# One group of 32 small grams in place of two groups of 16

## The chip, the cores and the metric

The kernel runs on one core of a Trainium2 chip. Such a core has a matrix engine (TensorE, PE in the profile, PEld for its weight loads), a vector engine (VectorE, DVE), a scalar engine (ScalarE, ACT), GpSimd (POOL) and SyncE (SP), each with its own queue of instructions, and 16 DMA engines. The engines wait for each other by semaphores. TensorE writes into PSUM, eight banks of 128 x 512 numbers, from which VectorE and ScalarE read. The metric is the device time of one execution in microseconds.

## The reference

One block of a streaming encoder on 512 tokens of width 1024, in float32: half a SwiGLU network, then two token mixers side by side (RWKV-7 and an attention with forget gates) that are gated and added, then another half SwiGLU and a last norm. The change lies in the RWKV-7 mixer, whose state follows this rule, per head of 64 channels, 8 heads:

```python
def step(state, inp):
    r_t, w_t, k_t, v_t, a_t, b_t = inp
    sa = jnp.einsum('bhvk,bhk->bhv', state, a_t)
    state = (state * w_t[:, :, None, :]
             + sa[..., :, None] * b_t[:, :, None, :]
             + v_t[..., :, None] * k_t[:, :, None, :])
    y_t = jnp.einsum('bhvk,bhk->bhv', state, r_t)
    return state, y_t
```

with a = -kk and b = kk * a, and w a decay below one.

## The kernel before, in words

The step over tokens is computed in chunks of 32. Within a chunk, the products of every token's a and r with every earlier token's b and k are needed: a small matrix of 64 x 64 per chunk and head, here called a gram. The 8 heads are held as 4 pairs, p = 0 to 3, a pair being 128 partitions, head q of it 64. There are 16 chunks, so a pair has 32 grams. `BK` holds b and k of a pair, both divided by the running decay; `G[p][q]` holds a and r times the running decay in head q's own 64 partitions. A gram takes BK's and G's 64 partitions of head q and writes 64 partitions of a PSUM bank, those of the *other* head. Two banks `gps` (named gp in the profile) hold the 32 grams, bank g the chunks 8g to 8g + 7. A masking on VectorE then multiplies 8 grams by a triangular mask and puts the result into G, into the 64 partitions that head q does not use. So a pair has four maskings. Each gram is two passes on TensorE, and the grams of the two heads run side by side in it.

Around the grams, `step(p)` computes what they need: columns of the input projection (`column`, `plain_gate`), each 24 full-size passes of 128 x 512 (lines 143 to 145: the weights' high part by the input's high part, then by its low part, then the low part of the weights by the high part of the input). A column's weights are loaded by SP into one of three buffers (raw), ScalarE rounds them (whi, line 135), VectorE takes the rest (wlo, line 136); whi and wlo have two buffers each. A column's bank (pk, pgt, two of them in turn) is emptied by VectorE: u (line 1205) or, for a gate, gs (line 1235), which POOL then stores. k is shaped on VectorE from kt of ScalarE (line 1266). The norm of kk is a sum by TensorE (khi, klo into pn, lines 1281 and 1282) and three steps on ScalarE (krn). `rk` goes another such way: rhi and rlo into pn (lines 1334 and 1335), times v as bon (line 1337), a bias on ScalarE, a store by SP to bsave.

After its maskings, POOL copies a pair's strictly lower part to Ld in memory (line 1324) and clears it in G. When all four pairs are there, Ld is read back as Ls (line 1348), and VectorE inverts 128 triangular matrices of 32 x 32 at once by 31 steps of a product (prod, line 1358) and a sum (TT, line 1360). Meanwhile TensorE computes the columns of the attention: v (pv), two gates, q and k (pq). Then qk is scaled, squared (qsq), rounded (h), and the rest (l) goes with it into the next sum, again on TensorE.

The order of the work: up to the end of the inverse, the framework's scheduler sets each engine's order, from its own estimates of when each instruction can run; `tc.issue_after(x)` forbids an instruction to stand before x, and the text's order decides what depends on what. From there on (`written(True)`, line 1460) VectorE, ScalarE and TensorE follow the order in which the code is written.

Of the kernel before, what the change touches and what calls it, by code (L numbers as in the profile page):

```python
# [50 lines left out]
def kernel(  # L51
# [39 lines left out]
    def bank(name, pool_=None):  # L91
        pool_ = pool_ or pm
        return pool_.tile([P, T], F32, tag="b", name=name)
# [70 lines left out]
    def split(dst_hi, dst_lo, src, hi_eng="act"):  # L164
        cast = act.copy(dst_hi, src) if hi_eng == "act" else dve.tensor_copy(dst_hi, src)
        return cast, dve.tensor_tensor(dst_lo, src, dst_hi.bitcast(F32), op=ALU.subtract)
# [127 lines left out]
    def pc(i):  # L294
        return par[:, i:i + 1]
# [345 lines left out]
    class Wide:  # L641
# [240 lines left out]
        def column(s, ps):  # L882
            s.rc = s.small[4]
            for i in range(2):
                pe.transpose(ps[:, i * P:(i + 1) * P], s.nrm.rstd[:, i * P:(i + 1) * P], ident[:])
            for i in range(2):
                dve.tensor_copy(s.rc[:, i:i + 1], ps[:, i * P:i * P + 1])
# [183 lines left out]
    with ExitStack() as mx:  # L1071
# [119 lines left out]
        def prep(name, p, n=T):  # L1191
            if p % 2 == 0:
                return alt[name]
            t = t2.tile([P, n], F32, name=name, tag=name)
            return t[:]

        def work(name, dt=F32):
            late = name in ("kka", "rk", "bon")
            return t2.tile([P, T], dt, name=name, tag="sb" if late else "sa", bufs=3 if late else 5)
# [40 lines left out]
        def plain_gate(m):  # L1240
            gate = Gate(m)
            gate.go()
            gate.out()
            return gate.mms
# [3 lines left out]
        def step(p):  # L1248
            if p % 3 == 0:
                k, r = spare[2], spare[3]  # L1250
            else:
                k, r = [t2.tile([P, T], F32, name=f"{n}{p}")[:] for n in "kr"]
            v = vs[p]
            cz, a = za[p]
            BK = BKs[p]
            if p:
                column(DA, p, k, 4)
            kk = prep("kk", p)
            act.activation(kk[:], k[:], AF.Copy, scale=pc(PAR_KK + p))
            sq = work("ksq")  # L1260
            act.activation(sq[:], kk[:], AF.Square)
            hi, lo = work("khi", F32R), work("klo", F32R)
            split(hi[:], lo[:], sq[:])
            t = work("kt")
            act.activation(t[:], a[:], AF.Identity, bias=nka[:, p:p + 1], scale=pc(PAR_KA + p))
            dve.scalar_tensor_tensor(k[:], t[:], 1.0, k[:], op0=ALU.add, op1=ALU.mult)
            with tc.issue_after(after[-1].ins) if after else ExitStack():
                dve.tensor_tensor_scan(cz[:], cmask[:], cz[:], initial=0.0, op0=ALU.mult, op1=ALU.add)
            Pp = prep("Pp", p, NC * (C + 1)).rearrange("p (c t) -> p c t", t=C + 1)
            pool.memset(Pp[:, :, 0:1], 1.0)  # L1270
            Pi = prep("Pi", p)
            with tc.issue_after(logs.ins):
                act.activation(Pi[:], cz[:], AF.Exp, scale=DEC)
                act.activation(Pp[:, :, 1:C + 1], ch(cz), AF.Exp, scale=-DEC)
            pool.tensor_copy(PC[:, p, :], Pp[:, :, C])
            after.append(dve.tensor_tensor(BK[:, :, 1, :], ch(k), ch(Pi), op=ALU.mult))

            mms = column(0, p, r, 0) if p else spread
            ps = bank("pn", pf)
            with tc.issue_after(mms[2].ins):  # L1280
                pe.matmul(ps[:], bonesr[:], hi[:], start=True, stop=False)
                pe.matmul(ps[:], bonesr[:], lo[:], start=False, stop=True)
            rn = work("krn")
            act.activation(rn[:], ps[:], AF.Relu, bias=tiny[:, 1:2])
            with tc.issue_after(logs.ins):
                act.activation(rn[:], rn[:], AF.Ln, bias=tiny[:, 0:1])
            act.activation(rn[:], rn[:], AF.Exp, scale=-0.5)
            dve.tensor_tensor(kk[:], kk[:], rn[:], op=ALU.mult)
            ka = work("kka")
            dve.tensor_tensor(ka[:], kk[:], a[:], op=ALU.mult)  # L1290
            dve.tensor_tensor(BK[:, :, 0, :], ch(ka), ch(Pi), op=ALU.mult)
            for q in range(2):
                s = slice(q * 64, (q + 1) * 64)
                dve.scalar_tensor_tensor(G[p][q][s, :, 0, :], ch(kk)[s], -1.0, Pp[s, :, 0:C],
                                         op0=ALU.mult, op1=ALU.mult)
            for q in range(2):
                s = slice(q * 64, (q + 1) * 64)
                dve.tensor_tensor(G[p][q][s, :, 1, :], ch(r)[s], Pp[s, :, 1:C + 1], op=ALU.mult)
            column(2 * DA, p, v, 8)
            mms = plain_gate(p)  # L1300


            gps = [pr.tile([P, 8, 2, C], F32, tag="b", name="gp") for _ in range(2)]
            for a_ in range(2):
                with tc.issue_after(mms[5].ins):
                    for c in range(8):
                        for q in range(2):
                            g = (a_ + q) % 2
                            s = slice(q * 64, (q + 1) * 64)
                            o = slice((1 - q) * 64, (2 - q) * 64)  # L1310
                            cc = g * 8 + c
                            gm = pe.matmul(gps[g][o, c], BK[s, cc], G[p][q][s, cc], start=True, stop=True)
                for q in range(2):
                    g = (a_ + q) % 2
                    o = slice((1 - q) * 64, (2 - q) * 64)
                    dve.tensor_tensor(
                        G[p][q][o, g * 8:(g + 1) * 8].rearrange("p c a t -> p c (a t)"),
                        gps[g][o].rearrange("p c a t -> p c (a t)"),
                        gmask[o].rearrange("p a t -> p (a t)").unsqueeze(1).broadcast_to([64, 8, 2 * C]),
                        op=ALU.mult)  # L1320
            for q in range(2):
                r0 = (1 - q) * 64
                un = (q * NP + p) * NC
                nc.gpsimd.dma_start(Ld[un:un + NC].rearrange("c s t -> s c t"), G[p][q][r0:r0 + C, :, 0, :])
                pool.memset(G[p][q][r0:r0 + C, :, 0, :], 0.0)


            rk = work("rk")
            dve.scalar_tensor_tensor(rk[:], r[:], pc(PAR_RK + p), k[:], op0=ALU.mult, op1=ALU.mult)
            ps = bank("pn", pr)  # L1330
            hi, lo = work("rhi", F32R), work("rlo", F32R)
            split(hi[:], lo[:], rk[:])
            with tc.issue_after(gm.ins):
                pe.matmul(ps[:], bonesr[:], hi[:], start=True, stop=False)
                pe.matmul(ps[:], bonesr[:], lo[:], start=False, stop=True)
            bon = work("bon")
            dve.tensor_tensor(bon[:], ps[:], v[:], op=ALU.mult)
            act.activation(bon[:], bon[:], AF.Identity, bias=pc(PAR_LB + p))
            nc.sync.dma_start(bsave[p], bon[:])

        for p in range(NP):
            step(p)
# [797 lines left out]
```

## Time and profile before

| | us |
|---|---|
| median of 3 runs | 1101.12 (1100.97 to 1101.41) |
| the profiled execution | 1101.58 |
| its span, first to last instruction | 1099.8 |
| TensorE busy in the span | 1090.9 |
| VectorE, ScalarE, POOL busy | 839.4, 669.3, 212.0 |
| one masking (16 of them) | 0.69 |
| first and last gram start at | 398.7 and 461.9 |

Times within the execution are counted from the start of the span. In rows of single instructions stand the start, the length, the engine and line, the operation, what is written from what is read, the shape, and in brackets how long the engine sat idle before and what ended it. Matmuls are pipelined, so their lengths overlap: what a pass takes is the distance to the next start.

### The profile page before, as it was taken

To read this page: it belongs to the slowest core of one execution; us is meant where nothing else is said; L and a number is where in the kernel's file an instruction comes from. 1 tells how busy PE (TensorE), PEld (TensorE's weight loads), DVE (VectorE), ACT (ScalarE), POOL (GpSimd) and SP (SyncE) were. 2 spreads that over 40 slices of the span, in tenths; PEclk is the share of its full clock that TensorE was granted. 3 is DMA by queue.
4 is the path that set the end of the run, shared out by engine and by line. 5 is a ranking of instruction groups with operands and counts; after the bars stand their busy time and mean duration, and the time that the engine had idled before them with its cause. 6 is when DMAs were issued, how large, how long until landed. Compare 5 with 4: busy or idle time off the path is not lost.

```text
span 1099.8 us, 16207 instructions
## 1 busy us (share of the span) xinstructions
PE 1090.9 (99%) x6050; PEld 889.6 (81%) x6050; DVE 839.4 (76%) x1162; ACT 669.3 (61%) x1046; POOL 212.0 (19%) x255
## 2 busy tenths in 40 slices
PE   9999999999999999999999999999999999999997
PEld 7888888888887888888777777888888888888886
DVE  7997676789756699779877666877697766789874
ACT  6765556575555765346887766533586555576554
POOL 1211221134204112311000121112311202114210
PEclk9999999999999999999999999999999999999999
DMA  7979887879926334445212244544968888859982
GB/s 221 252 166 240 199 179 200 191 146 189 236 91 186 110 101 121 115 134 125 58 34 72 77 139 147 175 132 155 284 151 190 188 218 170 184 158 204 235 189 77
DMA packets 139724, 177.09 MB, mean 161 GB/s; under 512 B 9726, under 2 KB 75838, under 8 KB 139646
## 3 DMA queue, kind: packets, MB, share of 16 engines
q0 software_dynamic: 33328, 70.40, 33.6%
q1 hardware_dynamic: 105582, 104.21, 31.0%
q10 hardware_dynamic: 736, 1.45, 0.3%
q8 instruction: 48, 0.79, 0.3%
q14 instruction: 30, 0.25, 0.1%
HBM read 163.51 MB, written 12.52 MB: 160 GB/s over the span
## 4 chain that ended last, share of the span: by engine, by line
PE 97%; ACT 1%; DVE 1%; DMA 0%; issue 0%; DVEq 0%; ACTq 0%
PE P L71 39%; PE P L144 5%; PE P L145 5%; PE P L143 5%; PE pgt L71 5%; PE lp L71 3%; PE pq L71 2%; PE pk L145 2%; PE ppj L71 2%; PE pk L143 2%; PE pk L144 2%; PE pb L71 2%; PE pa L71 1%; PE pw L144 1%; PE pw L145 1%; PE pw L143 1%
## 5 line engine op out<-in xcount | busy, mean ns | idle before, releaser
L71 PE MATMUL P<-sraw,q 128*128 128x512 f32 x344 | 91.3, 389 | 0.0
L135 ACT CAST whi<-raw 128x1024 fp32r<-128x1024 f32 (+3 forms) x43 | 41.1, 956 | 65.4 <-issue 19.3
L71 PEld LDWEIGHTS P<-sraw,q 128*128 128x128 f32 x344 | 64.6, 188 | 13.4
L71 PE MATMUL P<-swhi,q 128*128 128x512 f32 x224 | 71.5, 390 | 0.0
L71 PE MATMUL P<-sraw,wxh 128*128 128x512 f32 x200 | 68.4, 394 | 0.0
L136 DVE TENSOR_TENSOR wlo<-raw,whi 128x1024 fp32r<-128x1024 f32 (+3 forms) x44 | 49.6, 1127 | 17.8 <-ACT whi L135 16.6
L71 PE MATMUL P<-swhi,wxh 128*128 128x512 f32 x144 | 56.9, 395 | 0.0
L71 PE MATMUL P<-swhi,wxl 128*128 128x512 f32 x144 | 56.1, 390 | 0.0
L71 PE MATMUL P<-swlo,wxh 128*128 128x512 f32 x144 | 56.1, 389 | 0.0
L684 POOL DMA_DIRECT2D cb<-in_ffn_w_dram x20 | 24.1, 1204 | 151.3 <-DVE cd L71 85.6
L71 PE MATMUL P<-sraw,wxl 128*128 128x512 f32 x136 | 53.0, 390 | 0.0
L71 PEld LDWEIGHTS P<-swhi,q 128*128 128x128 f32 x224 | 42.0, 188 | 9.1 <-DVE q L71 0.5
L684 POOL DMA_DIRECT2D cd<-in_ffn_w_dram x24 | 29.5, 1229 | 102.6 <-DVE swlo L71 38.1
L71 PE MATMUL P<-swlo,q 128*128 128x512 f32 x112 | 43.6, 389 | 0.0
L71 PEld LDWEIGHTS P<-sraw,wxh 128*128 128x128 f32 x200 | 37.2, 188 | 7.3
L71 ACT CAST sraw<-cd 128x1024 fp32r<-128x1024 f32 x30 | 31.5, 1050 | 15.1 <-PE P L71 11.5
L71 DVE TENSOR_TENSOR swlo<-ca,swhi 128x1024 fp32r<-128x1024 f32 x24 | 29.2, 1222 | 13.9 <-ACT swhi L71 13.9
L71 DVE TENSOR_TENSOR u<-P,u 128x512 f32<-128x512 f32 x52 | 34.1, 685 | 5.8 <-ACT u L71 5.7
L71 DVE TENSOR_TENSOR swlo<-cc,swhi 128x1024 fp32r<-128x1024 f32 x20 | 24.5, 1224 | 18.1 <-ACT swhi L71 17.8
L543 POOL DMA_DIRECT2D ca<-in_ffn_w_dram x16 | 19.3, 1205 | 96.4 <-DVE swlo L71 66.4
L143 PE MATMUL pk<-xh,whi 128*128 128x512 f32 x96 | 37.8, 394 | 0.0
L145 PE MATMUL pk<-xh,wlo 128*128 128x512 f32 x96 | 37.5, 391 | 0.0
(613 smaller groups left out, 3451.6 us busy)
## 6 DMA issues: line engine op xcount, KB each, us to landing
raw<-in_w_in_dram SPq DMA_DIRECT2D x40, 512.0 KB
cc<-in_ffn_w_dram SPq DMA_DIRECT2D x36, 512.0 KB
cb<-in_ffn_w_dram POOLq DMA_DIRECT2D x36, 512.0 KB, 6.0
cb<-in_ffn_w_dram SPq DMA_DIRECT2D x32, 512.0 KB
cd<-in_ffn_w_dram POOLq DMA_DIRECT2D x32, 512.0 KB, 7.6
ca<-in_ffn_w_dram POOLq DMA_DIRECT2D x32, 512.0 KB, 7.1
ca<-in_ffn_w_dram SPq DMA_DIRECT2D x20, 512.0 KB
cd<-in_ffn_w_dram SPq DMA_DIRECT2D x18, 512.0 KB
```

The source lines that it names most:

```text
L71: q.last = do(*a, **kw)
L135: (hi_eng or act).copy(hi[:], raw[:])
L136: (eng or dve).tensor_tensor(lo[:], raw[:], hi[:].bitcast(F32), op=ALU.subtract)
L143: pe.matmul(ps, whi, xhi, start=first, stop=False, skip_group_check=onto)
L144: pe.matmul(ps, whi, xlo, start=False, stop=False, skip_group_check=onto)
L145: return pe.matmul(ps, wlo, xhi, start=False, stop=last, skip_group_check=onto)
L543: nc.gpsimd.dma_start(s.sum[g], src, accum_op=ALU.add)
L684: nc.gpsimd.dma_start(to, s.block(b, n, h), accum_op=ALU.add)
```

## The change

In `step`, the loop over the two groups (a_ = 0 and 1) held 16 grams and the two maskings of these 16. It is cut in two: a first loop issues all 32 grams, a second all four maskings.

```diff
             for a_ in range(2):
                 with tc.issue_after(mms[5].ins):
                     for c in range(8):
                         for q in range(2):
                             g = (a_ + q) % 2
...
                             gm = pe.matmul(gps[g][o, c], BK[s, cc], G[p][q][s, cc], start=True, stop=True)
+            for a_ in range(2):
                 for q in range(2):
                     g = (a_ + q) % 2
                     o = slice((1 - q) * 64, (2 - q) * 64)
```

The lines below move down by one, so that 1316 becomes 1317 and so on. What is computed is the same, and so are the instructions; the scheduler gives them another order.

TensorE at pair 0, before: from the last gram of the first group (G_2538 and G_2539 are the two heads of pair 0).

```order
L1312 MATMUL gp<-G_2539,BK_2546 64x64
L1281 MATMUL pn<-khi,bonesr 128x512
L145 MATMUL pgt<-xh_2478,wlo 128x512
L143 MATMUL pk<-xh_2587,whi 128x512
L144 MATMUL pk<-xl_2588,whi 128x512
L145 MATMUL pk<-xh_2587,wlo 128x512
```

TensorE at pair 0, after: from the last of the 32 grams.

```order
L1312 MATMUL gp<-G_2539,BK_2546 64x64
L1335 MATMUL pn<-rhi,bonesr 128x512
L1336 MATMUL pn<-rlo,bonesr 128x512
L1281 MATMUL pn<-khi,bonesr 128x512
L1282 MATMUL pn<-klo,bonesr 128x512
L145 MATMUL pgt<-xh_2478,wlo 128x512
L143 MATMUL pk<-xh_2587,whi 128x512
```

The second group stood 22 full-size passes after the first (khi and klo among them), with rhi and rlo behind it; now all four pn passes follow the 32 grams at once. In pairs 1 and 2 the 32 grams stand within three passes of the place of the former first group; in pair 3 they stand 15 passes of v behind it, which is before the place of the second.

VectorE at the same place, before: from the first two maskings of pair 0.

```order
L1316 TENSOR_TENSOR G_2538<-gp,gmask 64x512
L1316 TENSOR_TENSOR G_2539<-gp,gmask 64x512
L1235 TENSOR_TENSOR gs<-pgt,rstd 128x512
L1266 SCALAR_TENSOR_TENSOR k_2967<-kt,k_2967 128x512
L136 TENSOR_TENSOR wlo<-raw,whi 128x1024
L1276 TENSOR_TENSOR BK_2547<-k_2967,Pi 128x16x32
L1268 SCALAR_TENSOR_TENSOR BK_2549<-cmask,BK_2549 128x512
L1288 TENSOR_TENSOR kk<-kk,krn 128x512
```

And after, from the same neighbour (the row ahead of both is line 1096, V).

```order
L1266 SCALAR_TENSOR_TENSOR k_2967<-kt,k_2967 128x512
L1317 TENSOR_TENSOR G_2539<-gp,gmask 64x512
L1317 TENSOR_TENSOR G_2538<-gp,gmask 64x512
L1276 TENSOR_TENSOR BK_2547<-k_2967,Pi 128x16x32
L1317 TENSOR_TENSOR G_2538<-gp,gmask 64x512
L1317 TENSOR_TENSOR G_2539<-gp,gmask 64x512
L1268 SCALAR_TENSOR_TENSOR BK_2549<-cmask,BK_2549 128x512
L1338 TENSOR_TENSOR bon<-pn,V_2815 128x512
L1235 TENSOR_TENSOR gs<-pgt,rstd 128x512
L136 TENSOR_TENSOR wlo<-raw,whi 128x1024
L1288 TENSOR_TENSOR kk<-kk,krn 128x512
```

Four maskings and bon now stand ahead of gs and the weight split wlo, and k has come ahead of the maskings. The scan (line 1268) is listed as a SCALAR_TENSOR_TENSOR here.

VectorE at the end of the inverse, before: from the last weight split.

```order
L136 TENSOR_TENSOR wlo<-raw,whi 128x1024
L1358 TENSOR_TENSOR prod<-TT,Ls 128x87
L1360 TENSOR_TENSOR TT<-TT,prod 128x29x3
L1358 TENSOR_TENSOR prod<-TT,Ls 128x60
L1360 TENSOR_TENSOR TT<-TT,prod 128x30x2
L1358 TENSOR_TENSOR prod<-TT,Ls 128x31
L1360 TENSOR_TENSOR TT<-TT,prod 128x31
L71 TENSOR_TENSOR qk_3937<-qk_3937,rstd 128x512
```

And after.

```order
L136 TENSOR_TENSOR wlo<-raw,whi 128x1024
L1361 TENSOR_TENSOR TT<-TT,prod 128x30x2
L1359 TENSOR_TENSOR prod<-TT,Ls 128x31
L1361 TENSOR_TENSOR TT<-TT,prod 128x31
L71 TENSOR_TENSOR qk_3937<-qk_3937,rstd 128x512
```

Three more rows of the inverse now stand ahead of the split. Behind the inverse the order is the same in both kernels. SP issues the store of pair 0's bon one weight load earlier, and POOL copies pair 0's grams to Ld ahead of the store of the gate.

## The prediction

> **What bounds the kernel now.** I read the page's first and fourth parts, then TensorE's waits, then the windows around the grams, then the single instructions there. Page first (busy us, share of the span, count; then the chain by engine):
>
> ```profile
> PE 1090.9 (99%) x6050; PEld 889.6 (81%) x6050; DVE 839.4 (76%) x1162; ACT 669.3 (61%) x1046; POOL 212.0 (19%) x255
> ...
> PE 97%; ACT 1%; DVE 1%; DMA 0%; issue 0%; DVEq 0%; ACTq 0%
> ```
>
> TensorE is busy for 1090.9 of 1099.8 us and makes 97% of the chain that ends last. So only two things count: what TensorE executes, and where it waits. Its waits for other engines after the kernel's first microseconds (total, times, longest):
>
> ```profile
> PE pq L71 <- DVE l L71: 0.5, 1, 0.5
> PE pgt L71 <- DVE gs L71: 0.2, 1, 0.2
> ```
>
> No wait stands at the grams (L1312), only one later, for DVE's l. The windows over the stretch of the four pairs (length, then PE, PEld, DVE, ACT, POOL busy, clock, DMA share, GB/s):
>
> ```profile
> 398.60:410.00 11.40, 11.40 (x104) 9.33 (x104) 11.23 (x17) 6.50 (x9) 1.55 (x4) 1.00 0.40 114
> 410.00:420.00 10.00, 10.00 (x72) 8.12 (x71) 9.86 (x15) 5.91 (x9) 1.70 (x3) 1.00 0.53 146
> 420.00:430.00 10.00, 10.00 (x72) 8.14 (x71) 9.84 (x15) 6.53 (x9) 2.23 (x4) 1.00 0.33 93
> 430.00:437.00 7.00, 7.00 (x59) 5.65 (x58) 6.89 (x10) 3.29 (x5) 3.02 (x4) 1.00 0.45 124
> 437.00:450.00 13.00, 13.00 (x85) 10.60 (x84) 10.95 (x17) 7.40 (x10) 3.70 (x6) 1.00 0.35 107
> 450.00:470.00 20.00, 20.00 (x142) 16.24 (x141) 12.59 (x15) 6.90 (x9) 9.62 (x16) 1.00 0.44 119
> ```
>
> TensorE is full everywhere at clock 1.00. VectorE is nearly full too, up to 437: it has 0.17, 0.14, 0.16 and 0.11 us free, and only then 2.05 and 7.41 us. A lag that VectorE takes on at the first pair cannot be made good before 437.
>
> **Part 1: half of the changes between gram and full-size passes go.** TensorE at the first group of pair 0 (start, length, count; 32 instructions are 16 grams in two passes each), then the inside of that group:
>
> ```profile
> 398.13 0.39 PE L143 MATMUL pgt<-xh,whi 128*128 128x512 f32 x1
> 398.36 0.39 PE L144 MATMUL pgt<-xl,whi 128*128 128x512 f32 x1
> 398.68 1.15 PE L1312 MATMUL gp<-G,BK 64*64 64x64 f32 x32
> 399.76 0.50 PE L1281 MATMUL pn<-khi,bonesr 128*128 128x512 f32 x1
> 400.10 0.40 PE L145 MATMUL pgt<-xh,wlo 128*128 128x512 f32 x1
> ```
> ```profile
> 398.90 0.81 PE L1312 MATMUL gp<-G,BK 64*64 64x64 f32 x22
> ```
>
> Full passes follow each other every 0.23 us. Into the group it is 0.32, the group takes 1.08 to the next start, and the pass behind it 0.34: 1.74 us where two passes take 0.46, so a group costs 1.28. Inside, the 22 instructions are 11 side-by-side couples; the last starts at 398.90 + 0.81 - 0.22 (one gram lasts 0.22) = 399.49, ten steps of 0.059. A merged group of 32 grams then costs 1.28 + 16 x 0.058 = 2.21 against 2 x 1.28 = 2.56: 0.35 to 0.36 less a pair, 1.44 for four. The trace has no group of 32, so this is bounded: if the second half took its whole 1.08 again, only the steps in and out, 0.09 + 0.11 = 0.20 a pair, would go, 0.80 in all. I take 1.44, since the steady step is seen in the group itself. The same passes are issued; none is added or removed.
>
> **Part 2: VectorE's order, pair 0.** VectorE before, with the ScalarE instruction that it will meet:
>
> ```profile
> 398.56 0.69 DVE L166 TENSOR_TENSOR klo<-ksq,khi 128x512 fp32r<-128x512 f32 x1
> 399.17 0.74 DVE L1096 SCALAR_TENSOR_TENSOR V<-u,par,V 128x511 f32<-128x511 f32 x1
> 399.94 1.41 DVE L1316 TENSOR_TENSOR G<-gp,gmask 64x512 f32<-64x512 f32 x2
> 401.28 0.67 DVE L1235 TENSOR_TENSOR gs<-pgt,rstd 128x512 f32<-128x512 f32 x1
> 401.88 0.68 DVE L1266 SCALAR_TENSOR_TENSOR k<-kt,k 128x512 f32<-128x512 f32 x1
> 402.47 1.21 DVE L136 TENSOR_TENSOR wlo<-raw,whi 128x1024 fp32r<-128x1024 f32 x1
> 403.61 0.68 DVE L1276 TENSOR_TENSOR BK<-k,Pi 128x512 f32<-128x512 f32 x1
> 404.21 1.21 DVE L1268 TENSOR_TENSOR_SCAN BK<-cmask,BK 128x512 f32<-128x512 f32 x1
> ```
> ```profile
> 399.74 0.81 ACT L1265 ACTIVATE kt<-G,small,par 128x512 f32<-128x512 f32 x1
> ```
>
> In the new order k stands right behind V. It needs kt, which ends at 400.55, so VectorE idles from 399.91 to 400.6, where it masked before. Then, by the spacing of the starts above (a scan and a split alike, 1.14): k 0.60, two masks 1.34, BK 0.60, two masks 1.34, the scan 1.14, the bonus product bon 0.60, gs 0.60: the weight split wlo starts at 406.8 and ends at 408.05 (before: 403.68). TensorE reaches the column that uses it as follows: grams from 398.68, 2.00 long; the four pn passes 0.34 + 3 x 0.23, the last gate pass 0.23: the next column starts at 401.94 and, 24 passes later (5.44, by the distance of two whi in part 3), the one with this split at 407.4. Its third pass takes wlo as weights, and these are loaded one pass ahead, at 407.6. They come at 408.1. I enter **+0.4** with what a pass loses that starts after a wait (part 3). Bounds: 0, if kt or a mask is half a microsecond earlier than laid out, and 1.0, if VectorE is another 0.6 late.
>
> Pairs 1 to 3: VectorE carries the same instructions in both kernels, so its lag is no more than the idle 0.6 to 0.7 just added. Between this split and the next one behind a block of four masks, the new order has 21 instructions, 18.8 us at the same spacings; that split ends at 426.8, and TensorE loads it at 427.5. Some 0.6 us are spare, and more after 437. I enter 0 there; a further lag of 0.6 is the bound's other end.
>
> Other queues. POOL takes the two copies of pair 0 to Ld ahead of the gate's store, which then goes out about 6 us later; its buffer is wanted two gates on, over 20 us. SP puts the store of bon ahead of one weight load; bon is ready by 407.7 and that load waits for wlo (408.05) anyhow, and fills the third buffer ahead, first read past 420. On ScalarE bon slips between the logarithm and the exponential of pair 1's norm, 0.7 us. None reaches TensorE; the cover is the two or three columns (5.44 us each) by which loads run ahead.
>
> **Part 3: the triangular inverse starts earlier, and the wait for l goes.** The last masks of pair 3, the copies that they release, the inverse's first row:
>
> ```profile
> 462.49 1.41 DVE L1316 TENSOR_TENSOR G<-gp,gmask 64x512 f32<-64x512 f32 x2
> ```
> ```profile
> 463.47 1.36 POOL L1324 DMA_DIRECT2D Ld<-G  x2 [6.95 <-DVE G L1316]
> ...
> 467.81 0.57 POOL L1348 DMA_DIRECT2D Ls<-Ld  x1
> ```
> ```profile
> 472.00 0.19 DVE L1358 TENSOR_TENSOR prod<-TT,Ls 128x31 f32<-128x31 f32 x1 [2.50 <-DMA Ls<-Ld]
> ```
>
> Its two groups in the chain of waits (start, us to the next step):
>
> ```profile
> 453.82 1.08 PE gp L1312 x32
> ...
> 461.02 1.08 PE gp L1312 x32
> ```
>
> The one group of the new order stands 15 v passes behind the place of the first: 453.82 + 15 x 0.23 - 0.7 (three merges of 0.36, less the 0.4) = 456.5. It ends at 458.5, and four masks at 461.2 instead of 463.9. The chain to Ls then lands near 469.4, the inverse starts 2.5 us earlier and gets ahead of the weight splits between its rows. Its end, and the wait:
>
> ```profile
> 494.11 1.05 ACT L135 CAST whi<-raw 128x1024 fp32r<-128x1024 f32 x1 [3.91 <-PE pq L144]
> ...
> 499.55 1.06 ACT L135 CAST whi<-raw 128x1024 fp32r<-128x1024 f32 x1 [3.91 <-PE pq L144]
> ```
> ```profile
> 500.64 1.22 DVE L136 TENSOR_TENSOR wlo<-raw,whi 128x1024 fp32r<-128x1024 f32 x1 [0.39 <-ACT whi L135]
> ...
> 503.24 1.28 DVE L71 TENSOR_TENSOR qk<-qk,rstd 128x512 f32<-128x512 f32 x2
> ...
> 506.51 0.69 DVE L71 TENSOR_TENSOR l<-qsq,h 128x512 fp32r<-128x512 f32 x1
> ```
> ```profile
> 506.38 0.40 PE L71 MATMUL pq<-h,bonesr 128*128 128x512 f32 x1
> 507.26 0.50 PE L71 MATMUL pq<-l,bonesr 128*128 128x512 f32 x1 [0.48 <-DVE l L71]
> 507.60 0.40 PE L71 MATMUL pq<-xh,whi 128*128 128x512 f32 x1
> ```
>
> The pass with l starts 0.88 behind its forerunner in place of 0.23, and the next 0.34 in place of 0.23: the wait costs 0.65 + 0.11 = 0.76. Between the last split and qk lie 2.60 us: the split's 1.14 and six inverse instructions. Now three stand there, 0.7 to 0.8 less. TensorE is 1.1 earlier at that point (1.44 - 0.4), whi and its split with it, so that qk comes 1.9 earlier, at 501.4. l is then ready at 505.3, and TensorE asks for it at 506.6 - 1.1 = 505.5. **-0.76**, but narrowly; bounds 0 and -0.76.
>
> **Sum.** -1.44 + 0.4 - 0.76 = -1.8 us. From 508 on the orders are equal and TensorE stays full, so the gain is carried to the end. The profiled execution took 1101.58 (span 1099.8), 0.5 above the median 1101.12, hence 1099.8 for such an execution and **1099.3** for the median. 0.2% of it, 2.2 us, is about what a measurement of this kernel can tell from no change.
>
> **Rivals.** (B) VectorE keeps up: the idle before k is smaller, or TensorE's wait is hidden. Then -1.44 - 0.76 = -2.2, and the 0.2 wait for gs may shrink with it: 1098.7 to 1098.9. For it: my 0.4 hangs on one alignment. Against: the windows leave VectorE 0.17 us.
>
> (C) The wait for l stays, as the last split moves with TensorE; or a merged group saves only 0.20 a pair: -1.0 or -1.2, 1100 us. For it: l has 0.2 us in hand.
>
> (D) VectorE becomes the bound, and the kernel gets slower. Place: the block of four masks and bon, 2 x 1.34 + 0.60, ahead of gs and wlo in pairs 0 to 2; before, only two masks stood there. Where VectorE is late by a mask couple, bon and the idle before k, 1.34 + 0.60 + 0.70 = 2.6, and 0.7 is spare, a pair loses 1.9; three pairs lose 5.7, net +3.5: 1104.6. It decides once the three lose over 1.5 each (4.4 together, twice 2.2). For it: VectorE is 98% busy up to 437. Against: its work does not grow, and a lag is paid once, not each time. [...]
>
> That the scheduler undoes the merge is excluded: the order shows 32 grams in a row in all four pairs.
>
> **How the numbers follow.** Forecast 0.45, B 0.25, C 0.15, D 0.15. The forecast and C lie within 0.2%; B lies at or past the bound and I count it as faster; D is slower: 0.25, 0.60, 0.15. The range goes from 1098.3 (B with both small waits gone) to 1102.0 (VectorE's lag costing 2.7 us more than entered), leaving out most of D.
>
> **What would show it.** Right: L1312 in four groups of 64 instructions, each 2.0 us to the next start; a gap of 0.3 to 0.4 at 408 in front of an L145 pass, named by wlo; Ls read before 470; no wait for l. Wrong: merged groups longer than 2.1; TensorE waiting for u, gs or wlo in several columns between 400 and 450; l still waited for near 506.

## The result, and the profile after

The changed kernel took 1099.85 us (median of 21 runs, 1099.21 to 1100.38), the kernel before beside it 1101.23 us (21 runs): a ratio of 0.9986, 95% interval 0.9980 to 0.9993, or 1.4 us less. The experiments below ran in two series, each beside the kernel before: m123, m3, m012 and mkt in the first, the others in the second. In the second the changed kernel took 1099.63 against 1101.24, ratio 0.9984 (0.9975 to 0.9993). The forecast was 1099.3 us, within 0.2% of before, with 1098.3 to 1102.0 as its range. The difference is there, and it is smaller than the 0.2% that counted as a difference. Two runs of the second series, one of m03 and one of before, ran at a lower clock (0.90 and 0.75 on average) and are left out of all medians.

The profiled execution of the changed kernel took 1099.21 us, its span 1097.1. Its first gram starts at 398.11, where that of before starts at 398.68; the first 398 us are the same program and vary by some tenths from run to run. So 0.57 is added to its times below where they are set beside times of before, and the measure for all runs is the **distance** from the start of the first gram to the start of the pass behind the one with l. It was 507.60 - 398.68 = 108.92 before and is 505.31 - 398.11 = 107.20 after: 1.72 less.

First TensorE's busy time on the page, and its waits for other engines (total, times, longest):

```profile
PE 1088.8 (99%) x6050; PEld 889.5 (81%) x6050; DVE 839.1 (76%) x1162; ACT 668.2 (61%) x1046; POOL 212.6 (19%) x255
```
```profile
PE pgt L71 <- DVE gs L71: 0.2, 1, 0.2
PE pk L145 <- DVE wlo L136: 0.2, 1, 0.2
PE lp L71 <- ACT tr L71: 0.2, 1, 0.2
```

The wait for l is gone and one for wlo has come. The third row, in the attention behind the inverse, costs nothing: from the pass behind l to the start of the last pass are 585.10 us before and 584.93 after. TensorE around the grams of pair 0, and at the place of the new wait, there with the loading of the weights:

```profile
397.79 0.39 PE L144 MATMUL pgt<-xl,whi 128*128 128x512 f32 x1
398.11 2.08 PE L1312 MATMUL gp<-G,BK 64*64 64x64 f32 x64
400.12 0.50 PE L1335 MATMUL pn<-rhi,bonesr 128*128 128x512 f32 x1
400.46 0.39 PE L1336 MATMUL pn<-rlo,bonesr 128*128 128x512 f32 x1
...
407.09 0.39 PE L144 MATMUL pk<-xl,whi 128*128 128x512 f32 x1
407.66 0.50 PE L145 MATMUL pk<-xh,wlo 128*128 128x512 f32 x1 [0.18 <-DVE wlo L136]
408.00 0.39 PE L143 MATMUL pk<-xh,whi 128*128 128x512 f32 x1
```
```profile
407.66 0.19 PEld L145 LDWEIGHTS pk<-xh,wlo 128*128 128x128 f32 x1 [0.61 <-DVE wlo L136]
```

A group of 32 grams takes 400.12 - 398.11 = 2.01 to the next start, with 0.32 into it and 0.34 behind it. Less two passes at 0.23 it costs 2.21 us, and two groups of 16 cost 2 x 1.28 = 2.56: 0.35 less. The wait is read from starts too: 0.57 and 0.34 between the last three rows in place of 0.23 and 0.23, so 0.45 us. The 0.18 in brackets is smaller, since the lengths of passes overlap and the pass before still counts as busy up to 407.48. VectorE at the same place, and ScalarE:

```profile
398.60 0.74 DVE L1096 SCALAR_TENSOR_TENSOR V<-u,par,V 128x511 f32<-128x511 f32 x1
400.01 0.69 DVE L1266 SCALAR_TENSOR_TENSOR k<-kt,k 128x512 f32<-128x512 f32 x1 [0.67 <-ACT kt L1265]
400.62 1.38 DVE L1317 TENSOR_TENSOR G<-gp,gmask 64x512 f32<-64x512 f32 x2
402.04 0.69 DVE L1276 TENSOR_TENSOR BK<-k,Pi 128x512 f32<-128x512 f32 x1
402.76 1.41 DVE L1317 TENSOR_TENSOR G<-gp,gmask 64x512 f32<-64x512 f32 x2
404.09 1.21 DVE L1268 TENSOR_TENSOR_SCAN BK<-cmask,BK 128x512 f32<-128x512 f32 x1
405.22 0.66 DVE L1338 TENSOR_TENSOR bon<-pn,V 128x512 f32<-128x512 f32 x1
405.80 0.67 DVE L1235 TENSOR_TENSOR gs<-pgt,rstd 128x512 f32<-128x512 f32 x1
406.40 1.21 DVE L136 TENSOR_TENSOR wlo<-raw,whi 128x1024 fp32r<-128x1024 f32 x1
```
```profile
398.22 1.05 ACT L135 CAST whi<-raw 128x1024 fp32r<-128x1024 f32 x1 [1.93 <-PE pgt L144]
399.17 0.81 ACT L1265 ACTIVATE kt<-G,small,par 128x512 f32<-128x512 f32 x1
```

VectorE stands 0.67 us in front of k, and then brings wlo when TensorE already waits for it. The windows, first and later (length, then PE, PEld, DVE busy):

```profile
398.60:410.00 11.40, 11.21 (x97) 9.15 (x92) 10.63 (x16) 6.86 (x10) 3.58 (x6) 1.00 0.33 93
410.00:420.00 10.00, 10.00 (x99) 8.28 (x99) 9.88 (x15) 4.97 (x7) 0.13 (x1) 1.00 0.57 158
420.00:430.00 10.00, 10.00 (x45) 8.26 (x44) 9.93 (x15) 6.12 (x9) 2.56 (x5) 1.00 0.33 93
430.00:437.00 7.00, 7.00 (x86) 5.81 (x85) 6.99 (x11) 3.75 (x5) 2.39 (x2) 1.00 0.49 133
```

VectorE is idle for 0.77 us of the first window (0.17 before) and for 0.12, 0.07 and 0.01 of the next ones; TensorE waits in the first alone. Last, the grams of pair 3, the copies, the start and end of the inverse, and TensorE at the place of the old wait:

```profile
458.10 2.71 DVE L1317 TENSOR_TENSOR G<-gp,gmask 64x512 f32<-64x512 f32 x4 [2.55 <-PE gp L1312]
```
```profile
463.74 0.57 POOL L1349 DMA_DIRECT2D Ls<-Ld  x1
```
```profile
468.61 0.19 DVE L1359 TENSOR_TENSOR prod<-TT,Ls 128x31 f32<-128x31 f32 x1 [0.65 <-DMA Ls<-Ld]
...
499.10 1.23 DVE L136 TENSOR_TENSOR wlo<-raw,whi 128x1024 fp32r<-128x1024 f32 x1 [0.75 <-ACT whi L135]
...
500.87 1.28 DVE L71 TENSOR_TENSOR qk<-qk,rstd 128x512 f32<-128x512 f32 x2
...
504.15 0.69 DVE L71 TENSOR_TENSOR l<-qsq,h 128x512 fp32r<-128x512 f32 x1
```
```profile
504.85 0.39 PE L71 MATMUL pq<-h,bonesr 128*128 128x512 f32 x1
505.08 0.40 PE L71 MATMUL pq<-l,bonesr 128*128 128x512 f32 x1
505.31 0.39 PE L71 MATMUL pq<-xh,whi 128*128 128x512 f32 x1
```

l is ready at 504.15 + 0.69 = 504.84 and its pass starts at 505.08, 0.23 behind its forerunner: no wait, with 0.24 us in hand. (Before, the pass that waited started 0.06 behind the end of l, so of the 0.24 some 0.18 are slack.)

### The profile page after: what moved, and what is told of

Its sections match the earlier page's. It is cut to its first block, busy times and chain, and to the rows that moved or that the text cites. A ratio compares the mean times of both kernels' runs of the same rounds, so it can differ in the third digit from the quotient of the medians.

```text
span 1097.1 us, 16209 instructions
## 1 busy us (share of the span) xinstructions
PE 1088.8 (99%) x6050; PEld 889.5 (81%) x6050; DVE 839.1 (76%) x1162; ACT 668.2 (61%) x1046; POOL 212.6 (19%) x255
## 4 chain that ended last, share of the span: by engine, by line
PE 97%; ACT 1%; DVE 1%; issue 0%; DVEq 0%; ACTq 0%
PE P L71 39%; PE P L144 5%; PE P L145 5%; PE P L143 5%; PE pgt L71 5%; PE lp L71 3%; PE pq L71 2%; PE ppj L71 2%; PE pk L145 2%; PE pk L144 2%; PE pk L143 2%; PE pb L71 2%; PE pa L71 1%; PE pw L144 1%; PE pw L145 1%; PE pw L143 1%
```

## The experiments

All compare on the distance, since a part of 0.4 us does not show in a median whose runs differ by 0.7. For most of them the merge was made a choice of pairs: the loop body became two functions, and only the pairs in the list issue both groups of grams ahead of their maskings.

```diff
-            for a_ in range(2):
+            def grams(a_, cs=range(8)):
...
+                return gm
+            def masked(a_):
...
+            if p in (1, 2, 3):
+                steps = (grams, 0), (grams, 1), (masked, 0), (masked, 1)
+            else:
+                steps = (grams, 0), (masked, 0), (grams, 1), (masked, 1)
+            for do, a_ in steps:
+                gm = do(a_) or gm
```

| merged pairs | distance | wait near 407 | wait for l | median | ratio to before |
|---|---|---|---|---|---|
| none (before) | 108.92 | no | 0.76 | 1101.1 to 1101.2 | |
| 3 (m3) | 107.79 | no | no | 1100.06 | 0.9989 (0.9980 to 0.9998) |
| 1, 3 (m13) | 107.46 | no | no | 1099.74 | 0.9985 (0.9977 to 0.9994) |
| 1, 2, 3 (m123) | 107.10 | no | no | 1099.50 | 0.9985 (0.9977 to 0.9994) |
| 0, 3 (m03) | 107.94 | 0.45 | no | 1100.36 | 0.9992 (0.9983 to 1.0002) |
| 0, 1, 2 (m012) | 111.37 | 0.45 | far larger | 1105.90 | 1.0037 (1.0023 to 1.0050) |
| all (after) | 107.20 | 0.45 | no | 1099.85, 1099.63 | 0.9986, 0.9984 |
| all, kt first (mkt) | 106.74, 106.75 | no | no | 1099.48, 1099.46 | 0.9984 (0.9976 to 0.9993) |

**Pairs 1 to 3 (m123).** The list is `(1, 2, 3)`.

> Pairs 1 to 3 merged, pair 0 as before with two groups of 16. Measure: the distance from the first gram to the start of the pass behind l, which was 108.92 us in the kernel before (398.68 to 507.60) and 107.20 with all four pairs merged (398.11 to 505.31). Theory (a merged group saves 0.36; the gap near 407 comes from pair 0's four masks, bon and the idle before k ahead of one weight split; the wait for l goes because the inverse starts earlier): three merges 1.08, no gap near 407, no wait for l: 108.92 - 1.08 - 0.76 = 107.1, median about 1099.4. Rival (any merged block of masks makes VectorE late, the gap moves on to pair 1): 107.5, with a gap of 0.4 to 0.5 between 415 and 430.

The distance is 107.10, no wait is left near 407, and TensorE's waits hold neither wlo nor l. Beside the full change this kernel lacks pair 0's merge and is 0.10 better for it: there the merge's 0.35 buys a wait of 0.45.

**Pair 3 alone (m3).** The list is `(3,)`.

> Only pair 3 merged. Theory (its grams end earlier, so the inverse starts earlier and the wait for l goes): 108.92 - 0.36 - 0.76 = 107.8, median about 1100.1, no wait for l. Rival (the wait for l goes because TensorE's saved time lets its weight roundings come earlier, whatever pair 3 does): 108.5 or so, the wait for l stays at 0.4 or more.

The distance is 107.79, 1.13 below before, where 0.35 for one merge and 0.76 for the wait for l make 1.11. So the wait for l goes with pair 3's merge, through the earlier inverse: here pair 3's one group stands in the place of the former first, the inverse's first row stands at 466.26, against 472.00 before, its last row is done before the last weight split, and l ends 1.42 us ahead of its pass. From here to m123 two more merges bring 0.69, 0.345 each.

**Pairs 0 to 2 (m012).** The list is `(0, 1, 2)`.

> Pairs 0 to 2 merged, pair 3 with two groups, of which the second now stands 40 v passes into v where it stood 29 before. Theory: TensorE comes 1.08 - 0.45 = 0.6 to 0.7 earlier to l, but the inverse starts 1.8 later than before, and l is ready no earlier than before: the whole gain is given back, the wait for l grows from 0.65 to 1.5 or more, 109.2 (between 108.9 and 110.5), median 1101.0 to 1102.5. Rival (the wait for l does not hang on pair 3): 108.2, median about 1100.5.

The direction was right and the size wrong: 4.8 us more than before by the median. TensorE at pair 3's second group, VectorE's first row of the inverse, TensorE where the inverse's end is wanted, and windows there:

```profile
463.01 1.16 PE L1312 MATMUL gp<-G,BK 64*64 64x64 f32 x32
```
```profile
474.43 0.18 DVE L1369 TENSOR_TENSOR prod<-TT,Ls 128x31 f32<-128x31 f32 x1
```
```profile
505.73 0.39 PE L145 MATMUL pq<-xh,wlo 128*128 128x512 f32 x1
507.66 0.47 PE L71 MATMUL pq<-h,bonesr 128*128 128x512 f32 x1 [1.54 <-POOL RD L1516]
509.60 0.80 PE L71 MATMUL pq<-l,bonesr 128*128 128x512 f32 x1 [1.46 <-DVE l L71]
510.19 0.63 PE L71 MATMUL pq<-xh,whi 128*128 128x512 f32 x1
510.62 0.63 PE L71 MATMUL pq<-xl,whi 128*128 128x512 f32 x1
```
```profile
508.50:509.60 1.10, 0.01 (x1) 0.01 (x1) 1.07 (x3) 1.10 (x2) 0.93 (x2) 0.71 0.03 7
...
510.00:512.00 2.00, 2.00 (x6) 1.52 (x6) 1.95 (x4) 1.83 (x4) 1.82 (x3) 0.50 0.64 150
512.00:514.00 2.00, 2.00 (x6) 1.55 (x5) 1.91 (x4) 0.42 (x1) 0.00 (x0) 0.50 0.93 212
514.00:516.00 2.00, 2.00 (x6) 1.54 (x5) 0.30 (x1) 0.85 (x2) 0.00 (x0) 0.55 1.07 152
516.00:518.00 2.00, 2.00 (x10) 1.65 (x9) 0.75 (x1) 1.12 (x2) 0.00 (x0) 1.00 0.07 11
```

The second group of pair 3 comes later, as expected: it starts at 463.01, where before it was 461.02, which is 1.85 later as counted from the first gram. What the expectation missed is what follows. A weight split comes ahead of the inverse's first row, which stands at 474.43 instead of 472.00, and that lag stays to the end of the inverse: l, taken to be ready about as before, ends 2.2 us later from the first gram. Now not only l is late but also h, each by 1.70 us over the usual 0.23 (the row for h names POOL's RD, but ScalarE's h ends at 507.57, right ahead of the pass). And the granted clock falls to 0.50 within the second of these waits. Estimated from these windows as one step from 1.00 (503.00 to 505.60 has 1.00) to 0.50 and one back, the mean of 0.71 from 508.50 to 509.60 puts the fall at about 508.96, and the 0.55 of 514 to 516 puts its end at about 515.8: 6.8 us. In these, 13 passes from 510.19 to 515.74 take 0.43 each, 2.6 us more than at 0.23. In one of the five runs the mean clock of the execution was 0.999 and the time 1103.17 us, 2.7 below the median; in the other four it was 0.996 or 0.997, and 1105.01 to 1106.84. The 3.2 us from the pass at 505.73 to the fall held another pass at 507.66, between the two waits; what brings the clock down, and how that pass counted, no run shows.

**All four, with kt ahead of a weight rounding (mkt).** ScalarE's order before k is turned round: the rounding of one column's weights is kept behind kt.

```diff
+        def behind_kt(raw):
+            with tc.issue_after(kts[1].ins):
+                return split_w(raw, KD, P)
...
-            act.activation(t[:], a[:], AF.Identity, bias=nka[:, p:p + 1], scale=pc(PAR_KA + p))
+            kts.append(act.activation(t[:], a[:], AF.Identity, bias=nka[:, p:p + 1], scale=pc(PAR_KA + p)))
```

> All four pairs merged, and the weight rounding whi that stood ahead of kt on ScalarE at pair 0 put behind kt; nothing else changes up to the next column. Theory (the idle before k on VectorE makes the split late): k comes 0.4 to 0.5 earlier, the split too, the gap near 407 falls from 0.57 to 0.35 or less: 108.92 - 1.44 - 0.76 = 106.7 to 106.9, median about 1099.4. Rival (the split is late because of the four masks and bon themselves, and the early k only moves the idle in front of the masks): the gap stays at 0.5 to 0.6, 107.2.

ScalarE, VectorE and TensorE in this kernel:

```profile
399.11 0.81 ACT L1271 ACTIVATE kt<-G,small,par 128x512 f32<-128x512 f32 x1 [2.42 <-DVE klo L166]
399.83 1.03 ACT L135 CAST whi<-raw 128x1024 fp32r<-128x1024 f32 x1
```
```profile
399.95 0.69 DVE L1272 SCALAR_TENSOR_TENSOR k<-kt,k 128x512 f32<-128x512 f32 x1 [0.22 <-ACT kt L1271]
...
402.43 2.69 DVE L1325 TENSOR_TENSOR G<-gp,gmask 64x512 f32<-64x512 f32 x4
...
406.23 1.21 DVE L136 TENSOR_TENSOR wlo<-raw,whi 128x1024 fp32r<-128x1024 f32 x1
```
```profile
398.50 0.62 PE L1318 MATMUL gp<-G,BK 64*64 64x64 f32 x13
...
407.48 0.39 PE L144 MATMUL pk<-xl,whi 128*128 128x512 f32 x1
407.70 0.40 PE L145 MATMUL pk<-xh,wlo 128*128 128x512 f32 x1
```

VectorE idles 0.22 instead of 0.67, wlo starts 7.73 us behind the first gram instead of 8.29, and the wait is gone. The distance is 106.74, 0.46 below the changed kernel's. All four maskings now stand behind the scan, so the order moved too; what is shown is that the wait ends once wlo is half a microsecond earlier, of which the smaller idle is 0.45. It ends with little in hand: wlo is ready at 406.23 + 1.21 = 407.44, the loading for its first pass starts at 407.49 and that pass at 407.70.

**The changed kernel again, and mkt beside it (after_again, mkt_again).** Both unchanged, in one series.

> The change as it is, beside the others of this series. Theory (each merged group 0.35 less, one wait of 0.45 in pair 0, no wait for l): 107.2 us from the first gram to the start of the pass behind l, against 108.9 of the kernel before; the span about 1.7 us below that of the kernel before. The median differs by 1.4 in the first comparison, since the time around the span was 0.35 larger; if that belongs to the program, it is again 2.1 to 2.2 (before: 1.8) and the median differs by 1.4; if it was chance, the median now differs by 1.7.

> All four pairs merged, and ScalarE's kt put ahead of a weight rounding, beside the changed kernel itself. Theory: 106.7 against 107.2 from the first gram to the pass behind l, so about 0.46 below the changed kernel's span, and the median 0.4 lower. Rival (the time is made up elsewhere behind the inverse or around the span): the same median as the changed kernel within 0.1.

The distances repeat to 0.01: 107.19 and 106.75. (Of the other experiments there is one trace each.) The medians are 1099.63 and 1099.46, ratio of mkt to before 0.9984 (0.9975 to 0.9992). The 0.44 of the trace is 0.17 in the medians of this series; the earlier medians, 1099.85 and 1099.48, differ by 0.37 but come from different comparisons. The runs of each differ by 0.7 and more, so these medians neither confirm it nor speak against it. mkt is the best of the versions by its trace.

The time around the span, a run's time less its span, goes with the program and repeats between series: its median is 1.80 and 1.79 for before, 1.79 m3, 1.84 m03, 2.01 m123, 2.03 m13, 2.15 and 2.13 for the changed kernel (2.11 to 2.27), 2.15 and 2.17 mkt, 2.20 m012. What sets it stayed open: the traces begin alike, and none of them covers it.

**Pairs 1 and 3 (m13).** The list is `(1, 3)`.

> Only pairs 1 and 3 merged. Theory: two merges of 0.35 and the wait for l gone, no wait near 407, since the block of four masks stands in pair 0 no more: 107.4 from the first gram to the pass behind l. Rival (a lag of VectorE that any pair with four masks in a row passes on to the next column): a wait of 0.4 or more for wlo or gs appears behind pair 1, 107.8 or more.

The distance is 107.46. No wait for wlo is there, and for gs only the 0.2 in the attention that every version has: a block of four maskings in pair 1 passes nothing on to the next column.

**Pairs 0 and 3 (m03).** The list is `(0, 3)`.

> Only pairs 0 and 3 merged. Theory: the wait near 407 belongs to pair 0's own block (k waits for kt, then four masks and bon ahead of wlo) and stands there whatever the other pairs do: a gap of 0.55 to 0.6 between two passes near 407, and 108.79 less 0.70 less the rest of the wait for l, plus 0.45: 107.9 from the first gram to the pass behind l. Rival (the wait comes from the order of all four pairs): no gap, 107.4.

```profile
407.25 0.39 PE L144 MATMUL pk<-xl,whi 128*128 128x512 f32 x1
407.82 0.50 PE L145 MATMUL pk<-xh,wlo 128*128 128x512 f32 x1 [0.19 <-DVE wlo L136]
408.16 0.39 PE L143 MATMUL pk<-xh,whi 128*128 128x512 f32 x1
```

The gap of 0.57 stands here too, with pairs 1 and 2 as before, and the distance is 107.94. (The expectation's first number is a slip: from 108.92, less 0.70 and 0.76, plus 0.45, comes its 107.9.) The wait belongs to pair 0's own block.

## Why the prediction was right

- **The merge, -1.44.** Measured 2.01 for a group of 32, where 2.00 was laid out, and 0.345 a pair by m3 and m123: -1.38 for four. The lower bound, 0.20 a pair, is out: the second half of a merged group runs at the steady step, (2.01 - 1.08) / 16 = 0.058 a step.
- **The wait in pair 0, +0.4.** 0.45, at the pass, the time and the tile that were named. wlo was forecast to start at 406.8 and started at 406.40 + 0.57 = 406.97; the first two maskings took 1.42 to the next start, not 1.34. The prediction does not say from which point its 0.4 counts. From the loading of the weights, named at 407.6, to 408.1 and with 0.11 behind the wait it would be 0.6; from the pass's own place, 407.84, to 408.05 and with 0.11 it is 0.3. The trace shows the second way: loading and pass start together at 407.66, 0.34 behind the pass's place. So the time lost is right, while wlo's lateness was under-read by 0.13, and the agreement to 0.05 is in part luck. m123 and m03 tie the wait to pair 0's block, mkt to the lateness of wlo and, for the most part, to k waiting for kt.
- **Pairs 1 to 3, 0.** No wait there. The split behind pair 1's block ends at 426.9 in times of before (forecast 426.8) and is some 0.8 us ahead of the loading of its weights, where 0.6 was laid out. VectorE makes good 0.2 of its added 0.6 us up to 437 (0.20 us idle from 410, where before it had 0.41), and what is left of the lag delays no pass. Neither SP's nor POOL's moved issues reached TensorE: the starts hold no other stall.
- **The wait for l, -0.76.** Gone. In times of before, pair 3's maskings ended at 461.4 (forecast 461.2), the first row of the inverse stood at 469.2 (469.4) and qk at 501.44 (501.4). l had 0.24 us in hand, where 0.2 was laid out. m3 shows that it hangs on pair 3, m012 what lies on the other side.
- **The sum.** -1.38 + 0.45 - 0.76 = -1.69, and the distance fell by 1.72. The median span of the changed kernel was 1097.6 in the first comparison and 1097.4 in the second series; that of before was 1099.3 and 1099.4 in the two series: 1.7 to 2.0 less. The forecast -1.8 was of the span. The term that was not in it is the time around the span, carried over at 1.8 and measured at 2.13 to 2.15: about 0.35 us came back there, which is most of the 0.3 to 0.55 by which the median missed 1099.3. The prediction also took 2.2 us for about the least that a measurement can tell from no change; with 21 runs of each kernel the interval leaves no change out at a difference of 1.4 us.
- **The rivals.** B (VectorE keeps up) falls with the wait at 407, and the 0.2 for gs did not shrink. C falls on both its conditions. D (VectorE becomes the bound) falls as forecast: its lag was paid once. In the trace of after no wait stands at the grams (L1312); around them TensorE waits only for a weight split that is queued behind the maskings, 0.45 us.

## What to carry to other kernels

Each further group of small passes between full-size ones cost about 0.35 us here, so grouping pays about that, and the place to look is what the moved block makes late on the engine behind it. Read the slack of each join, not only the sum: l had 0.24 us in hand, the inverse without pair 3's merge lacked 3.4, and the same edit on different pairs gave from -1.6 to +4.8 us. Where an engine stands still for one operand at the head of a long block, as VectorE did here for 0.67 us in front of k, bring that operand's producer forward first: in mkt this took the 0.45 us of the wait away.

## What was not expected of the hardware

Within two waits of 1.70 us, with one pass between them, the granted clock fell to 0.50 and stayed there for some 6.8 us by the estimate above (13 passes at 0.43 us in place of 0.23, 2.6 us), so that, with the waits, a kernel with three merges and an inverse some 2.4 us later became 4.8 us slower. And the time around the span differed between programs that are alike but for the order of a few instructions, from 1.79 to 2.20 us, with single runs within some 0.1 of the median of each; for changes of a microsecond or two it has to be read beside the span.
